# Neighbourhood attention in fewer jobs, its room for outputs, and two operand pairs of the next set built early

## The chip, the cores and the metric

One NeuronCore of a Trainium2 chip runs the whole layer in one launch. The metric is the device time of one execution in microseconds (us), lower is better.

## What is computed

One encoder layer over 512 + 256 tokens of width 2048, float32. A modulation vector comes from `silu(c) @ w_ada`. Then:

```python
h    = rms(x, norm_g) * (1 + scl) + shift
proj = h @ w_in                       # pool_u, pool_z, q, k, v, attn_z, g_pool, g_attn
pool_y = pool_mixer(pool_u) * silu(pool_z)            # windows of 2, 4, 8, 16 and a 256x256 product per group
attn_y = neighbourhood_attention(rms(q), rms(k), v, rpb) * silu(attn_z)     # 16 heads of 64
merged = sigmoid(g_pool) * (pool_y @ w_pool_up) + sigmoid(g_attn) * (attn_y @ w_attn_up)
y = x + gate * (merged @ w_o)
```

## The kernel before

Features lie on the partitions (16 tiles of 128 for the width of 2048), the 768 tokens on the free axis in two halves of 384. Each float32 product is made of three TensorE products of a high and a low part (high x high, high x low, low x high). ScalarE (ACT) makes the high part with a cast, VectorE (DVE) the low part with a subtraction.

**Jobs.** `pair_job` computes two output tiles from eight tiles of the contraction with seven products in place of eight. The moving side of these products is a `Set`: four pairs of tiles, and for each pair the four operands B11, B12, B21, B22 (the halves themselves) and T1 to T4 (differences of halves, `differences`, lines 215 to 233). A job is 7 products of 12 matmuls (84), of 128x128 weights on 384 columns. Each set begins with an `opening`: two output tiles as plain products, 96 matmuls, which need the B operands alone. A later product of a job waits until its T operand is there for all four pairs.

**Sets, in order.** XA (first half of the contraction of the input projection, 38 jobs and some plain tiles), XB (second half, 39 jobs; its results are added to the stored first halves by a DMA that accumulates), XR (pooled output through `w_pool_up`), XY (attention output through `w_attn_up`), MA and MB (the two halves of `w_o`). XR, XY, MA and MB are one opening and seven jobs each.

**What sets the order.** The order of all instructions is written by the program itself. `run(n)` goes n steps through the products (a step is 6 matmuls, a job 14 steps). At each step `tick` issues what was planned for that step (`at`, `after`) and then `pump` takes at most one task from the list that `build` filled: fetch a pair of tiles (SyncE's DMA queue, SP), make it, put one operand. A task is taken only where `room()` (45 slots of 128x768 floats) leaves `heap["spare"]` slots free, and at a pace of one task in three steps (two in the last job of a set). `build(..., whole=w)` puts all eight operands of the first w pairs first; the other pairs get their B operands, and then the differences. A product whose operand is not there yet calls `need`, which issues tasks at once. Weights are split three products ahead (`prepare`, four buffers).

**The places that the change touches.**
- Lines 1001 to 1140: the `start` pool (the loads for the modulation), the jobs of XA, and `build(XB, ...)` with `x_pair` and `x_make` (lines 1125 to 1135): each pair of XB is loaded, normalised (L1134) and modulated (L998), and put.
- Lines 876 to 888: the list of XB's jobs. Per pair of heads p: one job for k and q, one for v and its gate, two for the merge gates (`gs`).
- Lines 549 to 683, `attention(p, start, pace)`: six units per pair of heads, one each `pace` steps. A unit's stages are planned in steps from its start: scores 0, bias and maximum 1, exponentials 3, transposes of v 5, their split 6, transposes of the weights 9, their split 10, values 13, output 14. Before them `norms` (lines 487 to 547) makes the norms of q and k: `sums` (TensorE), `take` one step later, `spread` (TensorE, the tile `yk`) four steps after that.
- PSUM: four banks for products, and one buffer each of the tags `s` (scores and `yk`, two banks), `pt` (transposes, and `n2`, the norms), `vo` (values).
- Lines 1175 to 1194: the attention's pool, the builds of XR and XY, the first loads of the gates (`sig_load`), and the pool `outs` of seven buffers, from which `output` takes a job's results once it is open.

The attention starts at step 25 after the pool `attn` opens and takes 56 steps for each of eight pairs of heads; 31 jobs of XB are left then, 434 steps.

Of the kernel before, what the change touches and what calls it, by code (L numbers as in the profile page):

```python
# [9 lines left out]
F32 = mybir.dt.float32  # L10
# [6 lines left out]
P = 128  # L17
D = 2048
KT = D // P
# [32 lines left out]
def encoder_layer(ctx: ExitStack, tc: tile.TileContext, xT, cT, w_ada2, w_ada4, b_ada, norm_g, w_in, pool_w,  # L52
# [98 lines left out]
    def after(n, fn):  # L151
        at(clock["now"] + n, fn)
# [334 lines left out]
    def norms(p, start):  # L487
# [9 lines left out]
                act.activation(flat(c["s" + nm]), flat(state[nm, p]), AF.Square)  # L497

        def sums():
            n2 = ps_aux.tile([P, 512], F32, tag="pt", name="n2")  # L500
            for i, nm in enumerate("kq"):
                for u in range(6):
                    pe.matmul(n2[:, 12 * i + 2 * u : 12 * i + 2 * u + 2], flat(c["s" + nm])[:, P * u : P * (u + 1)],  # L503
                              blk1[:, 0:P:64], start=True, stop=True)
            free(2)
            c["n2"] = n2[:, :24]
# [261 lines left out]
    def store_part(f):  # L768
        def go(i, t):
            pool.dma_start(part_d[f], flat(t))  # L770
            after(3, free)
        return go

    def merge_part(f):
        def go(i, t):
            pool.dma_start(part_d[f], flat(t), accum_op=ALU.add)
            after(3, free)
        return go

    def both(a, b):  # L780
# [78 lines left out]

    jobB = lambda a, b, da, db, last=False: pair_job(XB, cut(w_in, a, 1), cut(w_in, b, 1), both(da, db), last)  # L860
    GR = (3, 2, 1, 0)

    def pool_up(g):
        for i in range(2):
# [14 lines left out]
    for p in range(8):  # L879
        jobs.append((K0 + p, Q0 + p, qk_done("k", p), qk_done("q", p)))  # L880
        other = AZ0 + p
        jobs.append((V0 + p, other, v_done(p), fill(other)))
        for _ in range(2):
            a, b = gs.pop(0), gs.pop(0)
            jobs.append((a, b, fill(a), fill(b)))
    pair_jobs([jobB(*j, n == len(jobs) - 1) for n, j in enumerate(jobs[:1])])
    pool_up(GR[3])
    pair_jobs([jobB(*j, n == len(jobs) - 2) for n, j in enumerate(jobs[1:])])
# [11 lines left out]
    def pu_done(f):  # L900
        def go(i, t):
            sg = sig_take(f)
            dve.tensor_tensor(flat(t), flat(t), flat(sg), op=ALU.mult)
            pool.dma_start(mp_d[f], flat(t))
            free()
            release(t, 3)
            sig_load(f + 4)
        return go

    def au_done(f):  # L910
        def go(i, t):
            sg = sig_take(16 + f)
            dve.tensor_tensor(flat(t), flat(t), flat(sg), op=ALU.mult)
            free()
            if 16 + f + 4 < 32:
                sig_load(16 + f + 4)

            def add():
                pool.dma_start(flat(t), mp_d[f], accum_op=ALU.add)
                after(5, out)  # L920

            def out():
                pool.dma_start(merged_d[f], flat(t))
                state.setdefault("merged", set()).add(f)
                release(t, 3)
            add()
        return go
# [70 lines left out]
            dve.tensor_scalar(flat(t)[:, a:b], flat(t)[:, a:b], scale[:, kt, s : s + 1], shift[:, kt, s : s + 1],  # L998
                              op0=ALU.mult, op1=ALU.add)

    with tc.tile_pool(name="start", bufs=1) as sp_:
        ADABUFS = 5
        ada_list = [(g, i) for g in range(4) for i in range(8)]

# [81 lines left out]

        late = [(g, kt) for g in range(4) for kt in range(KT)]
        started = clock["now"]
        ready = {"pairs": 0}

        def late_load():
            if late:
# [15 lines left out]
        def late_out(g):  # L1108
            tr = turned(4)
            if g < 2:  # L1110
                modulation(4 + g, tr)
                ready["pairs"] = 2 * g + 2
            else:
                trv = tr[:, : 2 * P].rearrange("p (f j e) -> p j f e", f=2, j=4)
                cut_ = lambda z: z[:, 8 * (g - 2) : 8 * (g - 2) + 8].rearrange("p (j f) -> p j f", f=2)
                for s in range(2):
                    dve.tensor_tensor(cut_(gate[:, :, s]), trv[:, :, :, s], cut_(bada[:, 2]), op=ALU.add)
# [16 lines left out]
            dve.tensor_tensor(flat(t), flat(t), flat(rstd), op=ALU.mult)  # L1134
            apply(8 + 2 * j + (k == "b"), t)

        early = started + 14 * len(jobsA) - 100
        heap["spare"] = 4
        build(XB, x_pair, lambda j: j < ready["pairs"] and clock["now"] >= early, x_make, 0, 1)
        run(14 * len(jobsA))  # L1140


    with tc.tile_pool(name="mixp", bufs=1, reuse_waits="tile") as mp_:
        state["pool"] = mp_
        heap["spare"] = 6
        for i in range(2):
            state["u", i] = mp_.tile([P, PADW], F32, tag="u", name="u", bufs=2)
            pool.memset(state["u", i], 0.0)
        run(1)
        free()  # L1150
        run(16 + 8 * 14 + 4 * 4 - 1)

    def pooled(j):
        return stored(pooled_d, 2 * j)
# [20 lines left out]
    with tc.tile_pool(name="attn", bufs=1, reuse_waits="tile") as at_:  # L1175
        state["pool"] = at_
        act.preload_act_table_set(LNEXP)
        now = clock["now"]
        for p in range(8):
            attention(p, now + 56 * p + 25, 8)  # L1180
        run(31 * 14 - 40)
        build(XR, pooled)
        build(XY, attended, lambda j: state.get("attended", -1) >= 2 * j + 1, gated, 2, 1)
        run(40)
        for f in range(4):
            sig_load(f)
        run(16 + 2 * 14)


    outs["pool"] = ctx.enter_context(tc.tile_pool(name="outs", bufs=1, reuse_waits="tile"))  # L1190
    heap["spare"] = 1
    build(MA, lambda j: stored(merged_d, 2 * j), lambda j: {2 * j, 2 * j + 1} <= state.get("merged", set()), whole=2)
    build(MB, lambda j: stored(merged_d, 8 + 2 * j), lambda j: {8 + 2 * j, 9 + 2 * j} <= state.get("merged", set()), whole=2)
    run(5 * 14 + 3 * (16 + 7 * 14))


def _order():
# [88 lines left out]
```

## Time and profile before

| | us |
|---|---|
| three runs | 2067.04, 2068.19, 2069.83 |
| median | 2068.19 |
| the profiled execution | 2067.87 |
| its span, first to last instruction | 2066.1 |
| TensorE (PE) busy | 1949.3 (94%) |
| VectorE (DVE) busy | 1332.6 (64%) |
| ScalarE (ACT) busy | 1025.3 (50%) |
| GpSimd (POOL) busy | 259.6 (13%) |

The profile is of one execution; matmuls overlap in it, so that the busy time of PE does not tell how full it is. The number of matmuls in a stretch does: all products of a set have 384 columns, and a stretch that runs without waits shows what one takes. The granted clock stands beside it as a share of 2.4 GHz.

### The profile page before, as it was taken

To read this page: it belongs to the slowest core of one execution; us is meant where nothing else is said; L and a number is where in the kernel's file an instruction comes from. 1 tells how busy PE (TensorE), PEld (TensorE's weight loads), DVE (VectorE), ACT (ScalarE), POOL (GpSimd) and SP (SyncE) were. 2 spreads that over 40 slices of the span, in tenths; PEclk is the share of its full clock that TensorE was granted. 3 is DMA by queue.
4 is the path that set the end of the run, shared out by engine and by line. 5 is a ranking of instruction groups with operands and counts; after the bars stand their busy time and mean duration, and the time that the engine had idled before them with its cause. 6 is when DMAs were issued, how large, how long until landed. Compare 5 with 4: busy or idle time off the path is not lost.

```text
span 2066.1 us, 31567 instructions
## 1 busy us (share of the span) xinstructions
PE 1949.3 (94%) x11812; PEld 1834.4 (89%) x11812; DVE 1332.6 (64%) x2392; ACT 1025.3 (50%) x2207; POOL 259.6 (13%) x385
## 2 busy tenths in 40 slices
PE   3899999999999989999999999999979979999998
PEld 2889898888999879999999999999968968999997
DVE  5755555555566777756667666666766767677654
ACT  4433333333344344546556556556656555456653
POOL 0000000000000045410000100101100001112111
PEclk9999999999999989999999999999979999999999
DMA  9755555553333425555545545445634647767765
GB/s 354 258 189 182 200 189 202 191 189 138 136 138 134 154 57 143 133 126 119 126 97 127 119 105 127 109 115 125 172 119 151 246 157 191 226 162 197 207 174 142
DMA packets 100362, 331.92 MB, mean 161 GB/s; under 512 B 13169, under 2 KB 18289, under 8 KB 100209
## 3 DMA queue, kind: packets, MB, share of 16 engines
q1 hardware_dynamic: 68256, 217.35, 30.9%
q0 software_dynamic: 30944, 112.48, 23.4%
q8 instruction: 92, 1.51, 0.3%
q14 instruction: 62, 0.50, 0.1%
q10 hardware_dynamic: 1008, 0.09, 0.0%
HBM read 251.22 MB, written 78.64 MB: 160 GB/s over the span
## 4 chain that ended last, share of the span: by engine, by line
PE 81%; DVE 6%; ACT 5%; DMA 4%; issue 3%; POOL 0%; SPq 0%; ACTq 0%; POOLq 0%; DVEq 0%
PE acc L440 71%; PE acc L458 2%; PE adaacc L477 2%; PE op L662 1%; DMA adaw<-in_w_ada_dram 1%; DVE wlo L330 1%; ACT whi L329 1%; PE s L568 1%; PE n L503 1%; PE pt L629 1%; DMA wraw<-in_w_in_dram 1%; DVE sumsq L1031 1%; PE yk L539 1%; DMA in<-pooled_d 0%; DMA in<-merged_d 0%
## 5 line engine op out<-in xcount | busy, mean ns | idle before, releaser
L330 DVE TENSOR_TENSOR wlo<-wraw,whi 128x512 fp32r<-128x512 f32 (+1 forms) x357 | 249.1, 699 | 296.6 <-ACT whi L329 283.7
L330 DVE TENSOR_TENSOR wlo<-wsum,whi 128x512 fp32r<-128x512 f32 x420 | 293.6, 699 | 132.5 <-ACT whi L329 130.9
L440 PE MATMUL acc<-xbT,whi 128*128 128x384 f32 x1248 | 339.9, 353 | 10.5 <-DVE xbT L198 5.2
L329 ACT CAST whi<-wsum 128x512 fp32r<-128x512 f32 x420 | 260.6, 621 | 160.0 <-ACT whi L329 49.5
L440 PE MATMUL acc<-xaT,whi 128*128 128x384 f32 x1216 | 313.7, 338 | 1.1 <-ACT u L368 0.6
L329 ACT CAST whi<-wraw 128x512 fp32r<-128x512 f32 (+1 forms) x357 | 215.8, 605 | 116.1 <-PE acc L440 92.8
L368 ACT COPY u<-acc 128x384 f32<-128x384 f32 x210 | 100.5, 478 | 300.5 <-PE acc L440 300.5
L440 PE MATMUL acc<-xbB,whi 128*128 128x384 f32 x936 | 247.3, 345 | 0.5 <-DVE o L757 0.5
L440 PEld LDWEIGHTS acc<-xbT,whi 128*128 128x128 f32 x1248 | 229.9, 196 | 20.1 <-DVE xbT L198 7.4
L440 PE MATMUL acc<-xaB,whi 128*128 128x384 f32 x912 | 235.4, 339 | 0.0
L440 PEld LDWEIGHTS acc<-xaT,whi 128*128 128x128 f32 x1216 | 217.6, 188 | 16.2 <-issue 14.4
L440 PE MATMUL acc<-xbT,wlo 128*128 128x384 f32 x624 | 215.3, 345 | 0.0
L440 PE MATMUL acc<-xaT,wlo 128*128 128x384 f32 x608 | 203.9, 335 | 0.0
L440 PEld LDWEIGHTS acc<-xaB,whi 128*128 128x128 f32 x912 | 163.0, 188 | 11.9 <-issue 9.9
L440 PEld LDWEIGHTS acc<-xbB,whi 128*128 128x128 f32 x936 | 167.4, 191 | 4.4 <-issue 1.4
L440 PE MATMUL acc<-xbB,wlo 128*128 128x384 f32 x468 | 158.1, 338 | 0.0
L353 DVE TENSOR_TENSOR wsum<-wraw 128x512 f32<-128x512 f32 x210 | 145.4, 693 | 13.4 <-DMA wraw<-in_w_in_dram 13.2
L440 PE MATMUL acc<-xaB,wlo 128*128 128x384 f32 x456 | 153.0, 335 | 0.0
L353 DVE TENSOR_TENSOR wsum<-wsum,wraw 128x512 f32<-128x512 f32 x210 | 147.5, 702 | 0.0
L440 PEld LDWEIGHTS acc<-xbT,wlo 128*128 128x128 f32 x624 | 121.8, 195 | 0.0
L440 PEld LDWEIGHTS acc<-xaT,wlo 128*128 128x128 f32 x608 | 114.2, 188 | 0.0
L379 DVE SCALAR_TENSOR_TENSOR o<-u,acc 128x384 f32<-128x384 f32 x105 | 58.2, 554 | 85.8 <-ACT u L368 83.8
(252 smaller groups left out, 3435.9 us busy)
## 6 DMA issues: line engine op xcount, KB each, us to landing
wraw<-in_w_in_dram SPq DMA_DIRECT2D x160, 512.0 KB, 4.4
adaw<-in_w_ada_dram SPq DMA_DIRECT2D x96, 512.0 KB, 5.4
part_d<-o POOLq DMA_DIRECT2D x116, 384.0 KB, 2.8
wraw<-in_w_o_dram SPq DMA_DIRECT2D x32, 512.0 KB, 6.4
o<-part_d POOLq DMA_DIRECT2D x38, 384.0 KB, 4.8
sig<-part_d SPq DMA_DIRECT2D x32, 384.0 KB, 7.0
wraw<-in_w_pu_dram SPq DMA_DIRECT2D x16, 512.0 KB, 4.5
wraw<-in_w_au_dram SPq DMA_DIRECT2D x16, 512.0 KB, 5.9
```

The lines of the kernel that those rows point to most:

```text
L329: act.copy(hi[:, :n, :], raw)
L330: dve.tensor_tensor(lo[:, :n, :], raw, hi[:, :n, :].bitcast(F32), op=ALU.subtract)
L353: dve.tensor_tensor(t[:, :n, :], a, b, op=ALU.add)
L368: act.copy(t, c["a"][:, :TH])
L379: dve.scalar_tensor_tensor(c["o2"][:, 1, :], c["u3"], -1.0, c["c"][:, :TH], op0=ALU.mult, op1=ALU.subtract)
L440: pe.matmul(out, w, m, start=s["first"] and j == 0 and k == 0, stop=j == n - 1 and k == 2, skip_group_check=True)
L458: pe.matmul(c["ps"][h], w[:, j, :], mov[h][m], start=s["begin"] and j == 0 and k == 0, stop=last and k == 2, skip_group_check=True)
L477: pe.matmul(acc[32 * j : 32 * (j + 1), :n], cs[:, kt, :], w[:, n * j : n * (j + 1)], start=kt == 0, stop=kt == KT - 1)
L503: pe.matmul(n2[:, 12 * i + 2 * u : 12 * i + 2 * u + 2], flat(c["s" + nm])[:, P * u : P * (u + 1)], blk1[:, 0:P:64], start=True, stop=True)
L539: pe.matmul(c["b"][HALF[h], u // 3, P * (u % 3) : P * (u % 3 + 1)], src, ident, start=True, stop=True)
L568: pe.matmul(s[:, h, :K], a[HALF[h], q0 : q0 + P], b[HALF[h], key0 : key0 + K], start=i == 0, stop=i == 2)
L629: pe.transpose(pt[:n, j, h, :], c["p"][:, h, o_ : o_ + n], ident)
```

## The change

The jobs of XB are listed anew: for the first five pairs of heads (`DENSE`) one job for the merge gates comes with each pair in place of two, and the five jobs that are left over stand at the end. The attention follows: seven steps per unit for those five pairs, eight for the others. It is over at step 403 of the 434; then its pool is closed, the pool `outs` is opened, and XR's build begins with two whole pairs and one spare slot. The norms `n2` take the PSUM buffer of the scores. The gates are loaded two tiles ahead in place of four. In XA the pool `start` is closed once the modulation is made, and a pool `outs_a` of seven buffers takes the results of the last jobs; XB's build begins ten steps earlier, with two whole pairs and one spare slot in place of one pair and four.

```diff
         def sums():
-            n2 = ps_aux.tile([P, 512], F32, tag="pt", name="n2")
+            n2 = ps_aux.tile([P, 2, 512], F32, tag="s", name="n2")[:, 0, :]
...
     def store_part(f):
         def go(i, t):
             pool.dma_start(part_d[f], flat(t))
-            after(3, free)
+            release(t, 3)
...
+    DENSE = 5
...
-        for _ in range(2):
+        for _ in range(1 if p < DENSE else 2):
             a, b = gs.pop(0), gs.pop(0)
             jobs.append((a, b, fill(a), fill(b)))
+    while gs:
+        a, b = gs.pop(0), gs.pop(0)
+        jobs.append((a, b, fill(a), fill(b)))
...
-            sig_load(f + 4)
+            sig_load(f + 2)
...
-            if 16 + f + 4 < 32:
-                sig_load(16 + f + 4)
+            if 16 + f + 2 < 32:
+                sig_load(16 + f + 2)
...
-    with tc.tile_pool(name="start", bufs=1) as sp_:
+    with tc.tile_pool(name="start", bufs=1, reuse_waits="tile") as sp_:
...
-        early = started + 14 * len(jobsA) - 100
-        heap["spare"] = 4
-        build(XB, x_pair, lambda j: j < ready["pairs"] and clock["now"] >= early, x_make, 0, 1)
-        run(14 * len(jobsA))
+        modulated = 6 + 5 * KT * 4 + 8 * 4 + 6
+        run(modulated)
+
+    with tc.tile_pool(name="outs_a", bufs=1, reuse_waits="tile") as outs["pool"]:
+        early = started + 14 * len(jobsA) - 110
+        heap["spare"] = 1
+        build(XB, x_pair, lambda j: clock["now"] >= early, x_make, 0, 2)
+        run(14 * len(jobsA) - modulated)
+    del outs["pool"]
...
-        run(1)
+        run(16)
         free()
-        run(16 + 8 * 14 + 4 * 4 - 1)
+        run(8 * 14 + 4 * 4)
...
+        first = now + 25
         for p in range(8):
-            attention(p, now + 56 * p + 25, 8)
-        run(31 * 14 - 40)
-        build(XR, pooled)
-        build(XY, attended, lambda j: state.get("attended", -1) >= 2 * j + 1, gated, 2, 1)
-        run(40)
-        for f in range(4):
-            sig_load(f)
-        run(16 + 2 * 14)
+            attention(p, first, 7 if p < DENSE else 8)
+            first += 42 if p < DENSE else 56
+        done = first - 56 + 40 + 16 - now
+        run(done)
...
     heap["spare"] = 1
+    build(XR, pooled, whole=2)
+    build(XY, attended, lambda j: True, gated, 2, 1)
+    run(31 * 14 - done)
+    for f in range(2):
+        sig_load(f)
+    run(16 + 7 * 14)
```

On DVE, at the end of XA's last job, before the change. `xb` is a loaded tile of XB, `xbB` and `xbT` its operands, `wlo` the low part of a weight. The last `wlo` here is that of XB's fourth opening piece.

```order
L330 TENSOR_TENSOR wlo<-wraw,whi 128x512
L198 TENSOR_TENSOR xbB_6961<-xb,xbB_6961 128x384
L386 TENSOR_TENSOR o_6816<-acc,u_6904 128x384
L330 TENSOR_TENSOR wlo<-wraw,whi 128x512
L198 TENSOR_TENSOR xbB_6984<-xb,xbB_6984 128x384
L1134 TENSOR_TENSOR xb<-xb,rstd 128x768
L998 TENSOR_SCALAR xb<-xb,scale,shift 128x512
L998 TENSOR_SCALAR xb<-xb,scale,shift 128x256
L198 TENSOR_TENSOR xbB_7017<-xb,xbB_7017 128x384
L1134 TENSOR_TENSOR xb<-xb,rstd 128x768
```

And with the change, at the same `wlo`:

```order
L330 TENSOR_TENSOR wlo<-wraw,whi 128x512
L1136 TENSOR_TENSOR xb<-xb,rstd 128x768
L1002 TENSOR_SCALAR xb<-xb,scale,shift 128x512
L1002 TENSOR_SCALAR xb<-xb,scale,shift 128x256
L330 TENSOR_TENSOR wlo<-wraw,whi 128x512
L386 TENSOR_TENSOR o_6846<-acc,u_6939 128x384
L198 TENSOR_TENSOR xbT_6906<-xb,xbT_6906 128x384
L330 TENSOR_TENSOR wlo<-wraw,whi 128x512
L198 TENSOR_TENSOR xbB_7028<-xb,xbB_7028 128x384
```

Before, the second pair's B operands stand here and the third pair is still to be made; with the change the second pair is whole (its last T is `xbT_6906`) and the operands here are the third pair's.

On SP, the loads around the start of XR, before the change (`bias` is the attention's, `sig` the gates', `wraw` weights):

```order
L1160 DMA in<-pooled_d_204 128x768
L1160 DMA in<-pooled_d_205 128x768
L561 DMA bias<-in_rpb_dram 128x384
L307 DMA wraw<-in_w_pu_dram 128x1024 x2
L561 DMA bias<-in_rpb_dram 128x512
L307 DMA wraw<-in_w_pu_dram 128x1024 x2
L561 DMA bias<-in_rpb_dram 128x512
```

With the change:

```order
L1167 DMA in<-pooled_d_205 128x768
L1167 DMA in<-pooled_d_206 128x768
L307 DMA wraw<-in_w_pu_dram 128x1024
L897 DMA sig<-part_d_163 128x768
L897 DMA sig<-part_d_164 128x768
L307 DMA wraw<-in_w_pu_dram 128x1024
L1167 DMA in<-pooled_d_207 128x768
L1167 DMA in<-pooled_d_208 128x768
L1167 DMA in<-pooled_d_209 128x768
L1167 DMA in<-pooled_d_210 128x768
```

The bias loads are gone from here, two gates in place of four come with the opening, and the third and fourth pair (`pooled_d_207` to `210`) are loaded together, behind them.

On ACT, in XR's opening, before the change (`xrB`, `xrT` are XR's operands; L587, L598, L621, L642 and L670 are the attention's):

```order
L642 CAST ph<-pt 128x512
L194 CAST xrB_15646<-in 128x384
L587 ACTIVATE p,sm<-p,mx 128x256 x2
L194 CAST xrB_15668<-in 128x384
L194 CAST xrB_15688<-in 128x384
L329 CAST whi<-wraw 128x512
L670 COPY o<-op 64x128 x2
L621 CAST vh<-vt 128x128
L598 ACTIVATE p<-p,rc 128x256 x2
L194 CAST xrB_15713<-in 128x384
```

With the change:

```order
L194 CAST xrB_15858<-in 128x384
L194 CAST xrT_15868<-in 128x384
L329 CAST whi<-wraw 128x512
L194 CAST xrT_15886<-in 128x384
L194 CAST xrT_15895<-in 128x384
L194 CAST xrT_15905<-in 128x384
L329 CAST whi<-wsum 128x512
L194 CAST xrB_15928<-in 128x384
L194 CAST xrB_15932<-in 128x384
```

The attention's work is gone from XR's opening; in its place the second pair's T operands stand ahead of the third pair's B operands (`xrB_15928`).

## Rows read from the trace of the kernel before

**Rows 1.** The page: span, busy time of the engines, and the span in 40 slices of 51.7 us (busy tenths of PE, and the granted clock in tenths).
```profile
span 2066.1 us, 31567 instructions
PE   3899999999999989999999999999979979999998
PEclk9999999999999989999999999999979999999999
```

**Rows 2.** Matmuls by their moving operand, from the answers by tile: duration min/median/max in ns, first and last start in us. L458 is an opening, L440 the jobs.
```profile
L440 PE MATMUL acc<-xaB,wlo x456: 333/335/347, 97.8 to 704.5; 128*128 128x384 f32 x152
L458 PE MATMUL acc<-xbB,whi x64: 333/335/689, 704.7 to 727.5; 128*128 128x384 f32 x64
L458 PE MATMUL acc<-xrB,whi x64: 332/335/525, 1492.0 to 1518.0; 128*128 128x384 f32 x64
L458 PE MATMUL acc<-xyB,whi x64: 331/335/687, 1656.1 to 1681.2; 128*128 128x384 f32 x64
L458 PE MATMUL acc<-maB,whi x64: 333/335/689, 1809.0 to 1829.8; 128*128 128x384 f32 x64
L458 PE MATMUL acc<-mbB,whi x64: 333/334/335, 1934.9 to 1951.0; 128*128 128x384 f32 x64
L440 PE MATMUL acc<-mbB,wlo x84: 333/334/339, 1951.9 to 2056.6; 128*128 128x384 f32 x84
```

**Rows 3.** The chain of work that ended last, in order of time (start, length, what): a stretch of XA's jobs without a wait.
```profile
511.54 188.29 PE acc L440 x1086
```

**Rows 4.** Busy time of each engine by stretch (stretch, its length, then PE, PEld, DVE, ACT and POOL busy us with the number of instructions, granted clock, share of the DMA engines, GB/s): XB with the attention, then XR, XY, MA and MB.
```profile
900.00:1490.00 590.00, 585.34 (x3634) 553.56 (x3632) 387.62 (x786) 343.74 (x897) 56.26 (x68) 0.97 0.51 119
1492.00:1656.00 164.00, 144.33 (x753) 134.09 (x752) 113.49 (x202) 97.57 (x196) 9.00 (x16) 0.91 0.48 175
1656.00:1809.00 153.00, 131.07 (x686) 124.48 (x685) 109.08 (x182) 80.68 (x149) 21.56 (x30) 0.93 0.67 192
1809.00:1935.00 126.00, 122.53 (x687) 120.19 (x686) 87.67 (x155) 74.84 (x151) 23.49 (x33) 0.99 0.74 193
1935.00:2057.00 122.00, 119.44 (x685) 118.16 (x683) 73.14 (x125) 64.72 (x127) 23.48 (x33) 1.00 0.65 168
```

**Rows 5.** The same view, the starts of XB and XY.
```profile
704.70:755.40 50.70, 39.27 (x166) 33.92 (x164) 39.71 (x66) 19.15 (x40) 13.54 (x17) 0.80 0.32 88
1656.00:1712.00 56.00, 38.60 (x181) 33.17 (x179) 37.77 (x65) 29.56 (x53) 4.01 (x6) 0.90 0.49 158
```

**Rows 6.** DVE at the start of XB, in order of time (start, length, engine, line, operation, count, and in brackets the idle time before it and what ended it): making a tile, an operand, a difference, and a weight's low part.
```profile
711.12 0.68 DVE L330 TENSOR_TENSOR wlo<-wraw,whi 128x512 fp32r<-128x512 f32 x1
714.83 0.95 DVE L1134 TENSOR_TENSOR xb<-xb,rstd 128x768 f32<-128x768 f32 x1
715.82 0.87 DVE L998 TENSOR_SCALAR xb<-xb,scale,shift 128x512 f32<-128x512 f32 x2
718.84 1.96 DVE L198 TENSOR_TENSOR xbB<-xb,xbB 128x384 fp32r<-128x384 f32 x4
725.31 0.55 DVE L218 TENSOR_TENSOR xb<-xb 128x384 f32<-128x384 f32 x1
```

**Rows 7.** The same, later in that stretch, and POOL beside it.
```profile
736.22 1.86 DVE L198 TENSOR_TENSOR xbT<-xb,xbT 128x384 fp32r<-128x384 f32 x1
738.00 1.99 DVE L353 TENSOR_TENSOR wsum<-wsum,wraw 128x512 f32<-128x512 f32 x1
739.92 2.37 DVE L330 TENSOR_TENSOR wlo<-wraw,whi 128x512 fp32r<-128x512 f32 x1
735.82 5.92 POOL L712 TENSOR_TENSOR sum<-sum 128x797 f32<-128x797 f32 x3
```

**Rows 8.** TensorE's attention lines in XR (stretch, length, PE and PEld busy, clock, DMA): scores, values, transposes of the weights, transposes of v.
```profile
1492.00:1560.00 68.00, 2.07 (x18) 1.53 (x18) 0.81 0.35 119
1492.00:1600.00 108.00, 6.19 (x27) 5.14 (x27) 0.86 0.40 142
1492.00:1600.00 108.00, 2.91 (x19) 1.86 (x17) 0.86 0.40 142
1492.00:1600.00 108.00, 1.52 (x5) 0.58 (x5) 0.86 0.40 142
```

**Rows 9.** The chain of work, at the starts of XR, XY and MA: the loads that it waits for.
```profile
1495.97 10.15 DMA in<-pooled_d
1664.27 6.67 DMA in<-part_d
1810.91 9.84 DMA in<-merged_d
```

**Rows 10.** A unit of attention in XB, from PE's, ACT's and DVE's rows in order of time: transposes of the weights, their split, the transposes of v, the norms; then the scores and the bias; last, from the answers by line, all matmuls of the norms.
```profile
1052.05 0.60 PE L629 MATMUL pt<-ident,p 128*96 128x128 f32 x4
1055.54 0.74 DVE L647 TENSOR_TENSOR pl<-pt,ph 96x256 fp32r<-96x256 f32 x2
1057.56 0.31 PE L607 MATMUL vt<-ident,o 128*96 128x128 f32 x1
1060.43 3.18 PE L503 MATMUL n<-blk,sq 128*128 128x2 f32 x24 [0.45 <-DVE vl L622]
1063.65 0.18 DVE L511 TENSOR_SCALAR nx<-n 128x24 f32<-128x24 f32 x1 [1.71 <-PE n L503]
1079.27 0.27 PE L568 MATMUL s<-kl,qh 64*128 64x192 f32 x2
1080.22 0.74 DVE L577 SCALAR_TENSOR_TENSOR p<-s,ny,bias 128x192 f32<-128x192 f32 x2
L503 PE MATMUL n<-blk,sq x192: 167/251/354, 903.6 to 1456.9; 128*128 128x2 f32 x192
```

More of the change, by code (lines that the diff above doesn't have):

```diff
@@ L776, in go @@
             pool.dma_start(part_d[f], flat(t), accum_op=ALU.add)
-            after(3, free)
+            release(t, 3)
         return go
@@ L1088, in encoder_layer @@
         started = clock["now"]
-        ready = {"pairs": 0}
         def late_load():
@@ L1111, in late_out @@
                 modulation(4 + g, tr)
-                ready["pairs"] = 2 * g + 2
             else:
@@ L1178, in encoder_layer @@
         now = clock["now"]
+        first = now + 25
         for p in range(8):
-            attention(p, now + 56 * p + 25, 8)
-        run(31 * 14 - 40)
-        build(XR, pooled)
-        build(XY, attended, lambda j: state.get("attended", -1) >= 2 * j + 1, gated, 2, 1)
-        run(40)
-        for f in range(4):
-            sig_load(f)
-        run(16 + 2 * 14)
+            attention(p, first, 7 if p < DENSE else 8)
+            first += 42 if p < DENSE else 56
+        done = first - 56 + 40 + 16 - now
+        run(done)
     outs["pool"] = ctx.enter_context(tc.tile_pool(name="outs", bufs=1, reuse_waits="tile"))
     heap["spare"] = 1
+    build(XR, pooled, whole=2)
[4 more added lines that the diff above has]
+    run(16 + 7 * 14)
     build(MA, lambda j: stored(merged_d, 2 * j), lambda j: {2 * j, 2 * j + 1} <= state.get("merged", set()), whole=2)
     build(MB, lambda j: stored(merged_d, 8 + 2 * j), lambda j: {8 + 2 * j, 9 + 2 * j} <= state.get("merged", set()), whole=2)
-    run(5 * 14 + 3 * (16 + 7 * 14))
+    run(3 * (16 + 7 * 14))
 def _order():
```

## The prediction

> **What bounds the kernel now.** The page comes first: PE is busy 94% of the span, no other engine over 64%, and its row of slices is full except at the start, around slices 14 and 15, and in slices 29 to 36, where the granted clock falls too [rows 1]. So PE is the bound, and what can be won is where it starves. The tiles' first and last matmuls then cut the run into sets: XB's opening starts at 704.7, XR at 1492.0, XY at 1656.1, MA at 1809.0, MB at 1934.9, and MB ends at 2056.9 [rows 2]. What a set would take without waits follows from a stretch of XA without any: 1086 matmuls in 188.29 us, 0.1734 us each [rows 3]. XR, XY, MA and MB have 96 + 7 x 84 = 684 matmuls, 118.6 us. They take 164.1, 152.9, 125.9 and 122.0. XR has 69 matmuls of attention besides (753 against 684, [rows 4]); their four lines are busy for 2.1, 6.2, 2.9 and 1.5 us with ends that overlap [rows 8], so I take 11. Lost are then about 34 in XR, 34 in XY, 7 in MA, 3 in MB. At XB's start 166 matmuls (28.8 us) fill 50.7 us: 22 lost [rows 5]. From 900 to 1490, XB with attention, PE is busy 585 of 590 us [rows 4]: there its work is the bound, and nothing is lost but some 5 us.
>
> All four losses have one cause. When a set starts, its operands aren't made, and DVE and ACT make them while PE waits: in the 50.7 us at XB's start DVE is busy for 39.7, and the first 56 us of XY look the same, 37.8 on DVE and 181 matmuls, 24.6 us lost [rows 5]. MA, for which two pairs are put early, loses least of the three.
>
> **The change part by part.** The matmuls are the same, those of the attention too. Three or four jobs per pair of heads instead of four only move them: the 11 us of attention that now lie in XR are paid in XB, no gain and no loss. What counts is the waiting.
>
> *XB's start: 12 gained.* The second pair is now whole when XA ends. Off this stretch go two makings (0.95 + 0.87 each), eight operands at 1.96 / 4 = 0.49 and four differences at about 0.5 [rows 6]: 3.6 + 3.9 + 2.0 = 9.5 us of DVE, which is what PE waits for here. In XA the same work costs nothing, since the jobs there leave DVE a third or more of its time; this cover is gone only where it comes too late to be done by XA's end. Besides, three instructions of DVE between 736 and 742 take 1.86, 1.99 and 2.37 us while POOL adds [rows 7], where an operand takes 0.49 and a sum or a low part 0.68 [rows 6]: 6.2 against 1.9. With less to do ahead of them, part of them escapes: 2.5 more. Bounds: 5 (the opening's share alone, 23 us from 704.7 for 16.6 of matmuls, less what stays) and 19 (only MA's kind of loss is left). I take 12, the sum of the two.
>
> A rule bears on this. DVE's long instructions coincide with POOL's [rows 7]. The Trainium skill (SBUF — State Buffer, "SBUF: two separate sides") says that the pair of ports which DVE and GpSimd share is a lock, held for a whole instruction, and that the other blocks. The trace agrees in kind, with 2.37 us for 0.68. By that rule the fewer operands can still all meet POOL's three adds, and the sum would be 2.5 us less.
>
> *XR's start: 19 gained.* Attention ends at step 403 of 434, so DVE, ACT and SP are free of it in XR, and the first pair is built whole, the second fetched, before XB ends. But the third and fourth pair are fetched only within the opening, together, behind two weights and two gates on SP's queue; four tiles of 0.39 MB may land as late as the 10.15 us of the load that the chain waits for now [rows 9], against 8.3 us of matmuls that the first two pairs give. So the opening still waits some 3 us, and then eight T operands with their differences and two gates are made while PE needs them, another 7; the rest of XR keeps about 4. Bounds from the nearest sets: XY, without attention, still loses 34 (no gain); MA, which also has two pairs first, loses 7 (27 gained). XR is nearer to MA: its pairs need no making, no SiLU lies in its opening. I take 14 to 15 lost, 19 gained.
>
> *XY: 4 gained.* Its pairs come one to five steps earlier, the last fetch four steps earlier; the load that the opening waits for took 6.67 us [rows 9], and that wait shrinks by about that lead of 4 us. The T operands are in the same places. Bounds 0 and 9.
>
> *MA: 4 gained.* Its third and fourth pair are fetched four steps earlier and no longer behind the opening's weights; the wait for them took 9.84 us [rows 9]. Bounds 0 and its whole 7.
>
> *Attention closer together: 5 lost.* With seven steps per unit the transposes of v stand three steps after those of the weights instead of four, and both use the one buffer `pt`. The split of the weights ended at 1056.28, 3.6 us after the transposes at 1052.65 [rows 10]; three steps are 18 x 0.1734 = 3.1. Of 30 denser units perhaps 25 have such transposes: 0.2 us each. The norms in the scores' buffer: DVE takes them right behind their end (1063.65 for an end of 1063.61), and the bias reads the scores within 0.7 to 1.4 us of their end [rows 10], so at the next use one step (1.04 us) later little is waited for. Bounds: 0 and 15.
>
> *The rest: nothing.* Two gates in flight instead of four have a job of 14.6 us to land; the outputs' pool of seven holds three and a half jobs, and its room is free before the first output; both lie beside PE's work. If a gate landed late, ACT and behind it the split of the next weights would stand.
>
> Sum, against the profiled execution's 2067.87: 12 + 19 + 4 + 4 - 5 = 34, so **2034 us**. The median of the runs, 2068.19, is 0.3 above that execution, which changes nothing.
>
> **The rivals.**
> - *XR becomes a second XY.* The third and fourth pair land late and the T operands crowd ACT and DVE as they do in XY. For it: XY has no attention and loses 34; the two late pairs stand behind gates on SP. Against: nothing needs making. XR's 19 fall away: 2053. Chance 0.15.
> - *The starts close almost wholly*, as MB's does: XB's start gives 17, XR 25, XY and MA 8 together, the attention costs nothing: 2018 or less. For it: MB loses only 3. Against: it has idle ACT and DVE ahead of it, XB and XR haven't. Chance 0.12.
> - *The slower side: the attention's chain at seven steps.* If the split of the weights comes later than 4.6 us after the transposes (three steps and 1.5), PE waits 1.5 us in each of 30 units, 45 instead of 5, and the sum is 2034 + 40 = 2074. It decides at 34 / 30 = 1.1 us per unit above my figure. For it: the one at 1056.28 is already past three steps. Against: ACT and DVE are busy 58% and 66% there now [rows 4]. A pair of heads takes 79 us (from 903.6 to 1456.9 are seven of them, [rows 10]), 58.3 for its four jobs and 20 for attention; with three jobs it takes 64, and with the job that goes ACT and DVE lose its work too. Chance 0.05.
> - *The buffer of the scores.* PE's scores, norms and `yk` take turns in one buffer; were each turn held for DVE's 1.71 us [rows 10], 8 pairs of heads x 2 turns cost 27: 2061. The Trainium skill (Perfetto Trace Analysis, "Matmuls") wants independent groups to rotate through PSUM banks so that the evacuation of one overlaps the next; by it this edit is the wrong way round. That the old place waited too, 0.45 us for `pt`, speaks against a large price [rows 10]. Chance 0.03.
> - *It does not do what it says*: the new pools' first outputs wait for the pools whose room they take, and the early pairs slip into the opening as now: 2062 to 2068. Chance 0.03.
>
> **How the numbers follow.** The forecast keeps 0.62. A measurement of this kernel can tell 0.2%, 4 us, from no change. Faster are the forecast, the first two rivals and the buffer rival: 0.92, less 0.01 for their tails; within 0.2% lies most of the last rival and a mild form of the attention's: 0.04; slower 0.05. The forecast's own bounds reach from about 2022 to 2048; to leave out no more than 2 in 10 the range takes in the first rival and half of the second: 2015 to 2056.
>
> **What would show it.** Right: XR's own length falls from 164 to about 133 and holds no attention line; XB's opening starts at 704 to 706 as before and its next 160 matmuls end some 12 us sooner; XY and MA shorten by about 4 each; a pair of heads takes about 64 us in the dense part, with PE as full as now. Wrong: waits of PE for the split of the weights or for the norms within XB; a wait of XR's opening for `in<-pooled_d` of 8 us or more; an XR as long as 145; XB's start still at 50 us for 166 matmuls.

## The result, and the profile after

The changed kernel takes **2048.26 us** in the median of six runs (2041.39 to 2053.13), the kernel before 2067.97 on the same chip: a ratio of 0.9897, 95% interval 0.9874 to 0.9919. Forecast were 2034 us and a gain of 34; the gain is 20. The profiled execution took 2051.03 us.

The page of after, the lines that answer to [rows 1]:

```profile
span 2049.3 us, 31584 instructions
PE   3999999999999989999999999999989979999998
PEclk9999999999999999999999999999989989999999
```

The openings' first matmuls, from the answers by tile, as in [rows 2]:

```profile
L458 PE MATMUL acc<-xbB,whi x64: 334/334/689, 705.7 to 726.6; 128*128 128x384 f32 x64
L458 PE MATMUL acc<-xrB,whi x64: 334/334/687, 1500.1 to 1522.8; 128*128 128x384 f32 x64
L458 PE MATMUL acc<-xyB,whi x64: 334/334/522, 1643.1 to 1665.8; 128*128 128x384 f32 x64
L458 PE MATMUL acc<-maB,whi x64: 334/334/334, 1793.0 to 1809.1; 128*128 128x384 f32 x64
L458 PE MATMUL acc<-mbB,whi x64: 334/334/334, 1918.0 to 1934.1; 128*128 128x384 f32 x64
```

The difference of two starts is a set's length: XB 787.3 to 794.4, XR 164.1 to 143.0, XY 152.9 to 149.9, MA 125.9 to 125.0. XB is longer because the attention of XR, some 11 us, now lies in it. The gap to the forecast is above all in XR, which should have been about 133.

**XB's start.** The first 50 us hold 200 matmuls, where 166 stood in 50.7 [rows 5]. PE is idle in them for 10.5 us, hardly less than the 11.4 of before; what rose is the granted clock, from 0.80 to 0.90. That stretch, with the columns of [rows 5]:

```profile
705.70:755.70 50.00, 39.54 (x200) 37.18 (x200) 38.60 (x62) 21.50 (x46) 15.82 (x20) 0.90 0.33 85
```

What still stands there, from the rows in order of time of PE, ACT and SP (a bracket gives the idle time before an instruction and what ended it; an issue's length on SP includes its waiting):

```profile
746.04 1.01 PE L440 MATMUL acc<-xbT,whi 128*128 128x384 f32 x2 [4.93 <-ACT u L368]
...
745.00 0.62 ACT L329 CAST whi<-wraw 128x512 fp32r<-128x512 f32 x1 [2.98 <-DMA wraw<-in_w_in_dram]
745.52 0.47 ACT L368 COPY u<-acc 128x384 f32<-128x384 f32 x1
...
709.64 32.63 SPq L307 DMA_DIRECT2D wraw<-in_w_in_dram  x4
```

PE waits 4.93 us for a copy of a product (`u`). The copy takes 0.47, but on ACT it stands behind the split of a weight, and that weight has only just landed: its load was held on SP until a buffer came free at 742. Beside it DVE's stretched instructions are as they were [rows 7]:

```profile
735.38 1.86 DVE L230 SCALAR_TENSOR_TENSOR xb<-xb 128x384 f32<-128x384 f32 x1
737.17 1.86 DVE L198 TENSOR_TENSOR xbT<-xb,xbT 128x384 fp32r<-128x384 f32 x1
738.95 2.36 DVE L353 TENSOR_TENSOR wsum<-wsum,wraw 128x512 f32<-128x512 f32 x1
```

**XR's start.** What PE waits for from 1498 to 1560 (total, times, longest), then ACT and DVE in order of time:

```profile
PE acc L440 <- ACT p L368: 4.2, 1, 4.2
PE acc L458 <- ACT xrB L194: 3.2, 1, 3.2
PE acc L440 <- ACT u L368: 1.3, 1, 1.3
PE acc L440 <- DVE xrT L198: 1.2, 2, 0.7
```

```profile
1519.23 0.86 ACT L787 COPY po<-acc 128x384 f32<-128x384 f32 x2 [3.85 <-PE acc L458]
1520.11 1.28 ACT L901 ACT_TABLE_LOAD   x1
1521.41 0.85 ACT L901 ACTIVATE sig<-sig 128x768 f32<-128x768 f32 x1
...
1512.04 3.98 DVE L198 TENSOR_TENSOR xrB<-in,xrB 128x384 fp32r<-128x384 f32 x8 [1.08 <-ACT xrB L194]
1522.29 0.96 DVE L907 TENSOR_TENSOR po<-po,sig 128x768 f32<-128x768 f32 x1 [6.26 <-ACT sig L901]
1523.16 0.55 DVE L218 TENSOR_TENSOR in<-in 128x384 f32<-128x384 f32 x1
```

The third and fourth pair are there at 1512, the wait for them is 3.2 us. Then DVE stands for 6.26 us, with the differences of these pairs ready to be made, because next in its order is the gate's product of the opening's first output (L907). That product waits for the last matmul of this output (1519.2, four us before the opening ends), a copy, a table load and a sigmoid. Only at 1523.16 comes the first difference, and PE's wait of 4.2 comes behind it; the copy `p` that ends this wait stands on ACT behind the second gate's sigmoid and the operands' casts.

The waits are not the whole loss. PE's stretches (PE busy and matmuls, granted clock, DMA, GB/s):

```profile
1500.10:1510.10 10.00, 8.76 (x49) 1.00 1.01 274
1510.10:1520.10 10.00, 8.04 (x30) 0.66 0.57 226
1520.10:1530.10 10.00, 7.88 (x44) 1.00 0.10 40
1530.10:1540.10 10.00, 7.26 (x26) 0.66 0.23 73
```

Behind the wait of 3.2 us, 18 matmuls take 6.0 us (1512.06 to 1518.09), behind that of 4.2 us 18 take 5.9 (1532.84 to 1538.74): half the full rate, 1.2 in place of 2.4 GHz. At 0.1734 each they take 3.1. So each of the two waits costs nearly 3 us more than its own length.

**Attention.** All waits of PE from 900 to 1500 (6.5 us), and those of the kernel before from 900 to 1492 (4.6):

```profile
PE n L503 <- ACT sq L497: 2.1, 5, 0.4
PE yk L539 <- DVE ny L521: 1.4, 5, 0.4
PE vt L607 <- DVE pl L647: 1.3, 5, 0.3
PE vt L607 <- PE acc L440: 1.1, 5, 0.2
PE acc L440 <- ACT u L368: 0.6, 1, 0.6
```

```profile
PE n L503 <- DVE vl L622: 3.1, 7, 0.5
PE yk L539 <- DVE ny L521: 1.5, 5, 0.3
```

The transposes of v (`vt`) do wait for the split of the weights (`pl`), as expected, but five times and not 25. No price of the norms in the scores' buffer shows: `yk` waits as long as before, `n` less. In the dense part a pair of heads takes 65.6 us (the norms of the second to the sixth pair begin at 956.4 and 1218.7), where 64 were forecast.

### The profile page after: what moved, and what is told of

Same layout as the page of the kernel before. It is cut to its first block, busy times and chain, and to the rows that moved or that the text cites. A ratio compares the mean times of both kernels' runs of the same rounds, so it can differ in the third digit from the quotient of the medians.

```text
span 2049.3 us, 31584 instructions
## 1 busy us (share of the span) xinstructions
PE 1939.6 (95%) x11812; PEld 1832.7 (89%) x11812; DVE 1330.4 (65%) x2392; ACT 1023.1 (50%) x2207; POOL 259.8 (13%) x385
## 5 line engine op out<-in xcount | busy, mean ns | idle before, releaser
L440 PE MATMUL acc<-xbT,whi 128*128 128x384 f32 x1248 | 338.4, 352 | 10.6 <-ACT u L368 8.4
L440 PE MATMUL acc<-xaT,whi 128*128 128x384 f32 x1216 | 313.5, 338 | 1.1 <-ACT u L368 0.6
L440 PE MATMUL acc<-xbB,whi 128*128 128x384 f32 x936 | 245.7, 343 | 0.5 <-DVE o L757 0.5
L440 PEld LDWEIGHTS acc<-xbT,whi 128*128 128x128 f32 x1248 | 226.2, 194 | 19.3 <-ACT u L368 10.6
L440 PE MATMUL acc<-xaB,whi 128*128 128x384 f32 x912 | 235.3, 338 | 0.0
L440 PEld LDWEIGHTS acc<-xaT,whi 128*128 128x128 f32 x1216 | 217.5, 188 | 16.2 <-issue 14.4
L440 PE MATMUL acc<-xbT,wlo 128*128 128x384 f32 x624 | 214.8, 344 | 0.0
L440 PE MATMUL acc<-xaT,wlo 128*128 128x384 f32 x608 | 203.7, 335 | 0.0
L440 PEld LDWEIGHTS acc<-xaB,whi 128*128 128x128 f32 x912 | 163.0, 188 | 11.9 <-issue 9.9
L440 PEld LDWEIGHTS acc<-xbB,whi 128*128 128x128 f32 x936 | 165.7, 189 | 6.0 <-issue 1.4
L440 PE MATMUL acc<-xbB,wlo 128*128 128x384 f32 x468 | 157.2, 336 | 0.0
L440 PE MATMUL acc<-xaB,wlo 128*128 128x384 f32 x456 | 152.8, 335 | 0.0
L440 PEld LDWEIGHTS acc<-xbT,wlo 128*128 128x128 f32 x624 | 121.1, 194 | 0.0
L382 ACT ACTIVATE o<-acc 128x384 f32<-128x384 f32 x105 | 51.6, 492 | 125.3 <-PE acc L440 125.0
L440 PEld LDWEIGHTS acc<-xaT,wlo 128*128 128x128 f32 x608 | 114.1, 188 | 0.0
```

The costliest lines, as they stand in the source:

```text
L382: act.activation(c["o2"][:, 0, :], c["a"][:, :TH], AF.Copy, scale=-1.0)
L440: pe.matmul(out, w, m, start=s["first"] and j == 0 and k == 0, stop=j == n - 1 and k == 2, skip_group_check=True)
```

## The experiments

Five rounds each, in three groups (e1 to e4, e5 to e8, e9 to e12), each on one chip. Times are medians; the ratio is to the kernel before in the same group, so that runs of two groups are compared by their ratios. The lengths are those of the profiled execution, before: 787.3, 164.1, 152.9, 125.9.

| run | us | ratio, interval | XB | XR | XY | MA |
|---|---|---|---|---|---|---|
| e1 start only | 2057.13 | 0.9950 (0.9931 to 0.9968) | 774.8 | 163.8 | 153.0 | 125.9 |
| e2 attention only | 2054.22 | 0.9940 (0.9921 to 0.9959) | 799.4 | 139.9 | 150.5 | 122.1 |
| e3 again | 2044.81 | 0.9895 (0.9875 to 0.9914) | 795.8 | 140.1 | 150.5 | 122.0 |
| e4 gates late | 2042.15 | 0.9881 (0.9861 to 0.9901) | 790.4 | 135.8 | 150.5 | 124.8 |
| e5 weights' order | 2034.20 | 0.9843 (0.9827 to 0.9859) | 778.1 | 142.9 | 149.8 | 124.7 |
| e6 adds late | 2045.78 | 0.9902 (0.9886 to 0.9917) | 790.3 | 143.1 | 150.1 | 122.2 |
| e7 fetch early | 2043.39 | 0.9880 (0.9860 to 0.9900) | 786.6 | 139.6 | 150.0 | 122.2 |
| e8 e4, e5, e7 | 2029.05 | 0.9817 (0.9802 to 0.9832) | 778.6 | 135.5 | 146.0 | 123.9 |
| e9 before, weights' order | 2058.85 | 0.9963 (0.9949 to 0.9976) | 777.9 | 163.9 | 155.3 | 126.5 |
| e10 e8, adds late | 2024.12 | 0.9789 (0.9772 to 0.9806) | 780.2 | 136.4 | 143.3 | 122.3 |
| e11 e8, DENSE 7 | 2018.73 | 0.9764 (0.9750 to 0.9778) | 784.4 | 126.2 | 142.9 | 122.3 |
| e12 e8, DENSE 3 | 2024.94 | 0.9793 (0.9775 to 0.9810) | 772.9 | 146.4 | 143.0 | 122.3 |

**e1, the XA and XB part alone, and e2, all but it.** The diff of the change, cut in two at `with tc.tile_pool(name="start"` to `run(8 * 14 + 4 * 4)`.

> The kernel before with the XA and XB part alone: XA's loads leave early, a pool of outputs for its last jobs, two whole pairs of XB made there; attention and all that follows as before. Theory, from the two traces: the start gives 6 to 8 us (198 matmuls by 755.4 where 166 stood, 32 x 0.1734 = 5.5, and a little to 900), so 2060 to 2062. Rival, my forecast: 12 us, 2056; then some of it was lost again in XB after 900, in the attention.

> The changed kernel with XA and XB's start put back as before. Theory: the starts of XR, XY and MA give 10 + 3 + 1 and the denser attention costs 3 to 4, so 10 to 11 less than before: 2057 to 2058; the two halves add up to the whole, 2048 to 2050. Rival, my forecast: 19 + 4 + 4 - 5 = 22 less, 2046. In its trace XB (first opening matmul of XB to that of XR) is 787.3 + 11 of moved attention + the price of the denser attention: 801 to 802 by the theory, 803 by the forecast.

The group's before is 2065.44, so by the medians e1 gains 8.3 and e2 11.2, together 19.5 against e3's 20.6: the halves add within the noise. By its ratio e1 gains 10.3, and the interval, 6.6 to 14.3, holds both guesses. In its trace the first 100 us of XB have 477 matmuls where before has 421, which is 9.7 us. XB as a whole is 12.5 shorter, but its opening comes 3.0 later (707.7 against 704.7). So the start by itself is worth some 8 to 10, rather less than 12. e2's XB is 799.4, under both guesses; its gain, 11.2 or 12.4 by the ratio, rules out the forecast's 22 (interval 8.5 to 16.3).

**e3, the changed kernel again.**

> The changed kernel unchanged, a second time, for its spread and a second trace. Theory: the median is 2044 to 2050; the six runs on record lie between 2041.4 and 2053.1, wider than those of before. If a single place makes the difference between 2041 and 2051, the two traces differ there by most of it; if it is spread over the sets, no set differs by more than 3.

No single place: XB +1.4, XR -2.9, MA -3.0 against the first trace. What differs in MA is the clock. Both openings run without a wait, 100 matmuls from 1793 to 1810. PE's stretches behind them, the first trace and this one (PE busy and matmuls, granted clock, DMA, GB/s):

```profile
1810.00:1820.00 10.00, 6.57 (x34) 0.93 0.42 59
1820.00:1830.00 10.00, 10.00 (x54) 0.90 0.64 205
```

```profile
1810.00:1820.00 10.00, 7.97 (x46) 1.00 0.56 97
1820.00:1830.00 10.00, 10.00 (x60) 1.00 0.48 167
```

PE's one wait there, for the copy `p`, is 3.4 us in the first and 2.0 in the second. The first trace has 88 matmuls in 20 us, the second 106: 18 x 0.1734 = 3.1 us for a wait that is 1.4 longer. The rest, 1.7, went with the clock, 0.93 and 0.90 against 1.00.

**e4, XR's opening gates ten and twelve steps later.** `gate_` is the whole of the gate's work, which stood in `go`:

```diff
+        def go(i, t):
+            if f < 2:
+                after(10 if f else 12, lambda: gate_(t))
+            else:
+                gate_(t)
```

> The changed kernel; only the gates of XR's two opening outputs (sigmoid, product, DMA) are issued ten steps later, behind the T operands of the third and fourth pair. Theory: in XR the T operands wait for the gate's product, which stands ahead of them on DVE (idle 6.26 us for the sigmoid), not for late loads; XR falls from 143.0 by 5 to 9 and the time with it, 2040 to 2043. Rival, what I forecast: the late loads of the third and fourth pair and the mere number of T operands set it; then the gain is under 2, 2046 to 2048.

XR is 135.8, 4.3 under e3 and 7.2 under the first trace. The time is 2.7 under e3, with intervals that overlap, so XR's length is the witness. DVE's order and PE's waits from 1495 to 1555:

```profile
1511.07 0.55 DVE L218 TENSOR_TENSOR in<-in 128x384 f32<-128x384 f32 x1
...
1527.89 0.96 DVE L907 TENSOR_TENSOR po<-po,sig 128x768 f32<-128x768 f32 x1 [1.16 <-ACT sig L901]
```

```profile
PE acc L458 <- ACT xrB L194: 3.0, 1, 3.0
PE acc L440 <- ACT u L368: 2.6, 2, 1.8
PE acc L440 <- DVE xrT L198: 1.8, 1, 1.8
PE acc L440 <- ACT p L368: 0.7, 1, 0.7
```

The wait of 4.2 is 0.7 and the late load's 3.0 stays, but two others have grown, `u` to 2.6 and `xrT` to 1.8. In all of XR, PE is idle for 11.7 us, against 13.9 in e3 and 13.5 in the first trace. So only some 2 of the 4 to 7 us are waits; the rest is the clock, which stays up where the long wait was (compare 1530.10 to 1540.10 above):

```profile
1505.40:1515.40 10.00, 8.17 (x39) 0.83 0.37 146
1515.40:1525.40 10.00, 9.34 (x54) 1.00 0.00 0
1525.40:1535.40 10.00, 7.36 (x42) 1.00 0.79 259
```

e4 moves both gates at once. Whether DVE's 6.26 us at the first or the second gate's work on ACT, right ahead of the copy `p`, held PE is not told apart by it.

**e5, the U jobs' weights registered before the Z jobs'.**

```diff
-        zz = jobB(Z0 + f, ...)
+        uu = jobB(U0 + f, ...) if n else None
+        zz = jobB(Z0 + f, ...) if n else None
         if n == 0:
             opening(XB, ...)
-            pair_jobs([zz])
+            pair_jobs([jobB(Z0 + f, ...)])
         else:
-            pair_jobs([jobB(U0 + f, ...), zz])
+            pair_jobs([uu, zz])
```

> The changed kernel; in XB's first part the weights of the U jobs are registered, and so loaded, ahead of those of the Z jobs that follow them (now the Z jobs' come first and hold the four buffers, so that U's arrive when PE needs them). Theory: the 5 us that PE stands at 741 to 746 end with the load of the weights, and two milder places like it at about 786 and 823; the time falls by 4 to 8, to 2037 to 2041, and 50 us from XB's opening hold 215 matmuls or more, not 200. Rival, my forecast's stretched DVE instructions: POOL's adds at 733 to 741 set that place, and the load only lies beside them: less than 1.5 us.

The edit also puts the opening's weights ahead of those of the first Z job. The theory holds, and by more than it said: the time falls by some 11, the first 50 us hold 240 matmuls, and XB falls by 16 to 18 against the two traces of the changed kernel (by 12 and 8 against e4 and e7, whose XB is the same program: 786.6 to 795.8 is the spread of that length from run to run). That stretch, then PE's waits from 704 to 755:

```profile
706.00:756.00 50.00, 44.31 (x240) 42.70 (x240) 42.98 (x66) 25.28 (x50) 21.76 (x23) 0.97 0.38 94
```

```profile
PE acc L440 <- ACT p L368: 2.3, 1, 2.3
PE acc L440 <- DVE xbT L198: 1.6, 1, 1.6
PE acc L440 <- ACT u L368: 1.2, 1, 1.2
PE acc L458 <- DVE xbB L198: 0.5, 1, 0.5
```

The wait of 4.93 for `u` is 1.2. DVE's instructions beside POOL's adds are as stretched as ever (1.86 and 2.37 us at 733.9 and 735.7), and PE waits 1.6 us for a T operand.

**e6, the first mixing of U ten steps later.** `after(6 if f != 6 else 16, lambda: mix(f, t))`

> The changed kernel; the mixing of the first tile of U begins ten steps later, so that POOL's adds no longer lie beside the last T operands of XB's pairs. Theory A (POOL's adds stretch four DVE instructions from 2.5 to 7.4 us on the path of the T operands): 3 to 5 us less, 2040 to 2042. Theory B (the load of the weights ends last at 745 anyway): under 1.5 us, 2043 to 2046, and the stretched instructions only lie elsewhere.

Theory B: 2045.78, no other than e3 within the intervals. The adds do move, and DVE's T operands there take 0.55 us again. The first 50 us hold 219 matmuls, 13 to 21 more than in the first trace, e3, e4 and e7, which start alike without the edit, but the first 100 us hold 468, where those four have 461 to 480: what is won at the place is lost again behind it.

**e7, XR's pairs fetched before the second is put.** In `build`, for XR, pair 1 is fetched ahead of the first pair's puts, pair 2 ahead of its differences, and pair 3 ahead of the second pair's puts.

> The changed kernel; XR's third and fourth pair are fetched before the second is put, ahead of the gates on SP, and all else stays. Theory (late loads): the opening's wait for them, 3.2 us, goes and with it what the lower clock behind it costs: XR falls from 140 to 143 to 136 to 138, the time by 3 to 5. Rival (the gates' products ahead of the T operands): the wait only moves behind the opening, XR stays within 1.5 of 140.

The rival holds. XR is 139.6, against 140.1. The opening's wait for the high parts falls from 3.2 to 1.3, and the 4.2 behind the opening is still 4.2. PE is idle 1.7 us less in XR (12.2 against 13.9), and the clock is no better, 0.95 in both.

**e8, e4 and e5 and e7, and the gates late in XY too.**

> The changed kernel with the weights' order, the early fetch of XR's pairs, and the gates of the opening outputs ten steps later in XR and in XY. If the gains are of different places they add: 4 to 8, 3 to 5, 4 to 5 in XR and 2 to 4 in XY, so 2027 to 2033; XR 131 to 134, near the 133 of my forecast; XY 147 to 148. If the places of XR share one loss, 2033 to 2037.

2029.05 is within the first. XR, 135.5, is over the 131 to 134 expected, where the late gates alone had brought it (135.8): the early fetch adds nothing to its length. XY, 146.0, is 4 shorter, a little more than expected; its one long wait there, for the copy `p` behind the opening, falls from 6.8 to 2.4.

**e9, the kernel before with e5's edit.**

> The kernel before with the weights' order of XB's first part alone, as in the run on the changed kernel that fell by 11 us for it. Theory: in the kernel before the T operands are as late as the load, so that it wins less there: 4 to 7, 2059 to 2062; then the changed kernel's early operands had run into the load, and my 12 for XB's start was right but for it. Rival: the load is a loss of its own in both, 10 to 12 here too, 2054 to 2056; then the two add and my 12 was too high by itself.

Neither: 7.6 us less by the ratio, 9.3 by the medians. On the changed kernel the same edit gives 0.9895 - 0.9843, some 11. So the load was a loss of its own before, and the earlier operands ran into it by perhaps 3 more; the intervals, some 3 wide to each side, do not settle that.

**e10, e8 and e6's edit.**

> The kernel with weights' order, early fetch and late gates (2029.05), and the first mixing of U ten steps later. Theory: with the load out of the way POOL's adds beside the last T operands are next, 3.5 us of waits for the copies of the products and 1.6 for a T operand stand there: 2 to 4 less, 2025 to 2027. Rival: no more than on the changed kernel, under 1.5: 2028 to 2030.

The median is 4.9 lower, and the intervals overlap a little; but XB, where the edit acts, is 780.2 against 778.6, and the profile's gain lies in XY and MA, where it does nothing and where e11 and e12, of the same group and without the edit, are as short (143 and 122.3). I don't count it for POOL.

**e11 and e12, e8 with DENSE 7 and 3.**

> The same kernel (2029.05) with DENSE 7 in place of 5: attention is over 28 steps sooner, XR's build begins so much earlier, and 12 more units go seven steps. Theory (few waits per denser unit, 6.5 us in all of XB's attention): XR falls from 135.5 to 128 to 131, XB rises by 1 to 2, the time 2023 to 2027. Rival (each denser unit costs 0.4 us or more): XB rises by 5 or more, 2028 to 2032.

> The same kernel with DENSE 3: attention is over 28 steps later, four steps before XR's opening, and 12 fewer units go seven steps. Theory: the lead is what XR lives on; without it no pair is whole at the opening, XR rises to 142 to 150, XB falls by 1 to 2, the time 2034 to 2042. Rival (what XR gained came from the gates and the order of the T operands): XR within 3 of 135.5 and the time 2026 to 2031.

In e11 XR falls as the theory said and below it, and XB rises as the rival said; in e12 XR is as the theory said, and the time, 2024.94, is under both. The lead is what XR lives on: 146.4, 135.5, 126.2 us with DENSE 3, 5, 7. (The middle one is e8, of another group and chip; e10, with DENSE 5 and late adds, has 136.4 in the group of the other two.) XB goes the other way, 772.9, 778.6, 784.4, by more than the 1 to 2 of the theory. XB behind its first 200 us, DENSE 3, 5 and 7 (columns as in [rows 4]):

```profile
905.70:1478.60 572.90, 567.35 (x3545) 532.48 (x3544) 380.22 (x784) 342.86 (x916) 54.60 (x67) 0.98 0.50 117
```

```profile
906.60:1485.20 578.60, 572.15 (x3556) 535.47 (x3554) 386.12 (x796) 344.56 (x923) 54.88 (x66) 0.98 0.50 119
```

```profile
906.60:1491.00 584.40, 576.36 (x3554) 537.22 (x3553) 392.06 (x810) 347.71 (x933) 54.91 (x66) 0.97 0.50 119
```

The matmuls are the same to 0.3%; PE is idle for 5.5, 6.4 and 8.0 us. The mean of the clock over these stretches in tens of us is 0.982, 0.980 and 0.974; what is missing to 1 is 10, 12 and 15 us. From DENSE 3 to 7 idle time and clock make 2.5 and 5 of the 11.5; the rest stays open. Nor is the clock's share shown to be DENSE's: with DENSE 5 it was 0.974 in the first trace and 0.968 in e3. In e11 XR's opening needs no wait (its 64 matmuls of this row are all 334 ns):

```profile
L466 PE MATMUL acc<-xrB,whi x64: 334/334/334, 1491.0 to 1507.1; 128*128 128x384 f32 x64
```

e11, 2018.73, is the fastest here: 0.9764 of before.

## Why the prediction was right or wrong

The side was right and the time lies in the range, which was wide (2015 to 2056). The sum was 14 too large. Its terms, from the first trace and from e3:

| term | forecast | first trace | e3 |
|---|---|---|---|
| XB's start | 12 | 7.1 | 9.0 |
| XR's start | 19 | 10.1 | 13.0 |
| XY | 4 | 3.0 | 2.4 |
| MA | 4 | 0.9 | 3.9 |
| attention | -5 | -3.2 | -6.5 |
| XA's end and MB | 0 | -1.1 | -2.0 |
| sum (spans) | 34 | 16.8 | 19.8 |

XB's start is counted in matmuls 100 us behind the opening: 463 and 474 where before has 422, x 0.1734 (each a sum of two stretches). XR is its shortening less the 11 us of attention, an estimate. The attention is what is then left of XB.

What no term of the sum holds is the clock. The forecast counted all that PE lost as waiting and set the new losses by waits alone. Here the length of a stretch is parted into its matmuls at 0.1734 us, the time in which PE is idle, and the rest; the rest is about the share that the granted clock is under 1:

| stretch | length | matmuls | PE idle | rest | clock |
|---|---|---|---|---|---|
| XB's first 100 us, before | 100.0 | 73.0 | 13.9 | 13.1 | 0.88 |
| the same, first trace | 100.0 | 79.9 | 13.1 | 7.0 | 0.93 |
| the same, e3 | 100.0 | 81.8 | 10.8 | 7.3 | 0.93 |
| the same, e5 | 100.0 | 89.8 | 6.8 | 3.3 | 0.98 |
| XR, before (with 11 of attention) | 164.1 | 129.6 | 19.7 | 14.8 | 0.91 |
| XR, first trace | 143.0 | 118.6 | 13.5 | 10.9 | 0.93 |
| XR, e3 | 140.1 | 118.6 | 13.9 | 7.6 | 0.95 |
| XR, e4 | 135.8 | 118.6 | 11.7 | 5.5 | 0.97 |

- *XB's start: mis-sized, and not by the mechanism given.* The failed sentence is "which is what PE waits for here". After the operands came early PE stood 4.93 us for a copy behind a weight that was not loaded, and e5 took that away. So PE waited only 0.8 (first trace) to 3.1 us (e3) less, where 12 were forecast; some 6 us came back by the clock, for which no term stood. The 2.5 us that should escape POOL's adds did not: three instructions are as long as before. The port rule weighed in the prediction (the Trainium skill, SBUF — State Buffer, "SBUF: two separate sides") agrees in kind with 2.36 us for 0.68. What it would take off the sum, those 2.5 us, did fail to come; but e6, which moves the adds away, shows no gain in the time from it.
- *XR's start: the term that failed most.* The late load was sized right, 3 us forecast, 3.2 seen. For the T operands and gates I took 7 us, and the waits behind the opening are 6.7 there; all of XR has 13.5 us of idle PE where I took 14 to 15 lost. Lost are 24. But they are not waits for the number of operands: I counted their work and not their order. DVE stands idle for 6.26 us behind a product that waits for ACT, e4 shows that the place of the gates makes the wait of 4.2, and e7 that the load is not it. And each long wait costs the clock behind it, 10.9 us in all in the first trace, 7.6 in e3, put at nothing in the sum. That the waits alone came out at the forecast's size is in part luck. The Trainium skill (PSUM — Partial Sum Buffer, "Engine vs sequencer instructions") calls the queues of ScalarE, VectorE and GpSimd strict FIFO. DVE's 1522.29 ahead of 1523.16 is such a queue's head.
- *XY and MA.* Of the right order, but not by the waits named. XY's opening waits 4.4 and 3.9 us for operands where it waited 5.4; its longest wait, 6.8 us for the copy `p`, stayed until e8 put the gates late. MA's opening had waits of 1.3 us to lose and has none; it gained 0.9 or 3.9 by the clock behind one wait.
- *Attention: the size right, the reason not.* The transposes of v wait for the split, 1.3 us in all where 5 were taken. A pair of heads took 78.7 us before; without the job that goes (14.6) that would be 64.1, and it takes 65.6 in the first trace, 65.7 in e3, 65.1 in e8 and 65.2 in e11. That is 1.0 to 1.6 us for six units, 5 to 8 for the thirty. PE's waits in XB are only 1.6 to 1.9 us longer than before; what makes up the rest is not shown.
- *The scores' buffer: nothing, as said.* Its rival, 2061, did not come. The rule on rotating PSUM banks (the Trainium skill, Perfetto Trace Analysis, "Matmuls") spoke for that rival; no run here shows a price of breaking it.

Of the signs named in the prediction, the pair of heads at about 64 us is there, and none of the waits in XB that were to be large. XR at 143 lies between its two signs, 133 and 145. XB's first 160 matmuls end 5 us sooner, not 12.

## What to carry to other kernels

When operands are made earlier, ask of each engine at that place not how busy it is but what stands at the head of its order: a product that waits for a sigmoid, or a split that waits for a load, holds everything ready behind it. Loads go out in the order in which buffers are claimed, so claim them in the order of use. A lead is worth most where it is long enough for the opening to find all operands made: 28 steps more were worth 10 us in XR, of which XB, 6 us longer in these traces, took more than half. Price a wait with the clock behind it.

## What was not expected of the hardware

The same kernel's runs spread by 12 us with the mean granted clock: 2041.39 and 2041.77 us at 0.978, 2051.03 at 0.973, 2053.13 at 0.971. In XB's attention PE's waits are 6.5 and 6.2 us in the two traces of the changed kernel, none over 0.6, while the stretches in which the clock falls are in part others. A wait has two prices, its length and what the clock costs behind it, and the second was nearly 3 us behind each of XR's two, of 3.2 and 4.2 us; it was 1.3 to 1.7 us in MA for one wait of 3.4 us (27 matmuls short of the 115 that 20 us hold are 4.7 us; the clock's two rows say 1.7) and nothing for one of 2.0 (9 short, 1.6 us).
